# Reordering the end of each retention group: gate products, outputs and output transposes

## The chip, the cores and the metric

The kernel runs on one core of a Trainium2 chip. The metric is the device time of one execution in microseconds (us), lower is better; several executions are timed and their median is compared. The engines are named as in the profile: PE is TensorE, DVE is VectorE, ACT is ScalarE, POOL is GpSimd, SP is SyncE, which here only issues DMAs.

## The reference

One layer of a bidirectional encoder, 1024 tokens by 1024 features, float32. After a modulated RMS norm, one input projection feeds two head groups. Group A is retention: 8 heads with 64-wide q and k and 128-wide v, each in chunks of 128 tokens, a forward and a backward direction, then a group norm per head and a SiLU gate. Group B is latent attention. Both go through one output projection. The change touches group A and the gate of group B:

```
rq, rk = rope(r_q), rope(r_k) * dk ** -0.5
scores = einsum('bhnik,bhnjk->bhnij', qc, kc) * decay_intra
out    = einsum('bhnij,bhnjv->bhniv', scores, vc) + (qc * q_decay) @ states   # chunkwise, both directions
o      = (o - mean(o)) * rsqrt(var(o) + EPS) * ret_gn_w                       # per head, over its 128 columns
ret_out = o * silu(r_g)
mla_out = rms_norm(att) * silu(m_g)
```

## The kernel before

All large products are made in three parts, from high and low halves of both operands: mm3 (L64 to L67) issues high x high (L65), high x low (L66) and low x high (L67). The normalised input is held as hh[k] and hl[k], k = 0 to 7 (128 features by 1024 tokens each); weight pages are loaded by SP, split by ACT (L80) and POOL (L81) and held in a ring of 7.

Retention works in four groups g of two heads (the loop at L333). In each group:

- For each of eight token tiles t, 24 products (8 k by 3 parts, 512 columns) make q, k and v of the tile in one acc bank. ACT copies v out (L348); DVE multiplies q and k by the cosine and sine tables into t1 and t2 (L357, L359), two buffers each; POOL sums them into one of two rotary buffers rb (L363, L364). Then comes the retention step of the tile: PE transposes q, k and a copy into a bank tp of tag sm (L372, L373), DVE and ACT make the halves (L375 to L385), PE makes the scores scp (mm3, L387) and the chunk's states kv (L394), in a bank of tag sm each, and DVE and ACT carry the states on (L389 to L410). In group 0 the products of all eight tiles are already made in the start stage.
- The gate: two heads by two halves of the tokens, 24 products each into an acc bank (in the profile `acc<-hh,wh`; a retention product is `acc<-wh,hh`), then ACT's Silu into sg (L423). sg has one buffer.
- The outputs, for each half of the tokens: four tiles, each with four matmuls into a bank op of tag sm (L433, L434), ACT's copy to o (L436, five buffers), DVE's statistics (L439, L440); POOL makes the power -0.5 (rstd, L61 and L62); DVE normalises in eight instructions (L446); PE transposes eight blocks into two tp banks of tag sm (L451); DVE multiplies with weight and gate into ro (L453, two buffers); SP stores ro to retD in DRAM (L455).

After the four groups, mla_gate(0) and mla_gate(1) make the gates of the attention heads in the same way, 24 products to an acc bank and a Silu into mo (L469), stored by ACT's queue (L470). For these two, mo has the tag ro: it shares the two buffers with the ro of the outputs.

PSUM has eight banks: four of tag acc, four of tag sm.

The order in which each engine issues its instructions is set by a planner when the program is built. It goes through the program by priority, which is the order of the source, takes what its own model holds ready, and fixes the order; each engine then follows its own queue in order, and waits at the head. A tile of a tag gets one of the tag's buffers when one is free. So in the profile products of later stages run ahead of earlier stages' waiting work: the gate products of a group at its beginning, and those of the next group's tiles between the retention steps.

`tc.issue_after(ins)` adds an edge of order alone: what the block issues on the engine of `ins` is queued behind `ins`.

Of the kernel before, what the change touches and what calls it, by code (L numbers as in the profile page):

```python
# [9 lines left out]
F32 = mybir.dt.float32  # L10
# [3 lines left out]
ALU = mybir.AluOpType  # L14
# [4 lines left out]
P = 128  # L19
D = 1024  # L20
S = 1024
KT = D // P
# [8 lines left out]
def body(tc, I, O):  # L31
    nc = tc.nc
    V, A, G, T, SY = nc.vector, nc.scalar, nc.gpsimd, nc.tensor, nc.sync
# [16 lines left out]
    ident = ctile("ident", P)  # L50
# [13 lines left out]
    def mm3(out, lh, ll, rh, rl, first, last, **kw):  # L64
        T.matmul(out, lh, rh, start=first, stop=False, **kw)  # L65
        T.matmul(out, lh, rl, start=False, stop=False, **kw)  # L66
        T.matmul(out, ll, rh, start=False, stop=last, **kw)  # L67

    p_lat = None
    s_h = ExitStack()  # L70
# [24 lines left out]
    def sm(n=512):  # L95
        return pp.tile([P, n], F32, name="sm", tag="sm", bufs=8 - NACC)

    hh = [p_h.tile([P, S], F32R, name=f"hh{k}", tag=f"hh{k}") for k in range(KT)]
    hl = [p_h.tile([P, S], F32R, name=f"hl{k}", tag=f"hl{k}") for k in range(KT)]
# [3 lines left out]
    ts_ = lambda t: slice(t * P, (t + 1) * P)  # L103
# [162 lines left out]
    for h in range(H):  # L266
# [17 lines left out]
                    in1=posf.unsqueeze(2).broadcast_to([P, NT, 32]), op=ALU.mult)  # L284
# [44 lines left out]
    for z_ in qz:  # L329
        for b_ in z_:  # L330
            G.memset(b_.bitcast(F32), 0.0)

    for g in range(4):  # L333
        w = w0 if g == 0 else [wpage(I["w_ret"][g][j], 1024, 2) for j in range(4)]
        vv = []
# [3 lines left out]
        for t in range(NT):  # L339
            if g == 0 and t < NB0:  # L340
                ps = acc0[t]
            else:
                ps = acc()
                for k in range(KT):
                    wh, wl = w[k // 2]
                    mm3(ps, hh[k][:, ts_(t)], hl[k][:, ts_(t)], wh[:, k % 2], wl[:, k % 2], k == 0, k == KT - 1)
            v_ = p_ret.tile([P, 2, P], F32, name="v", tag="v", bufs=9)
            A.copy(out=v_.rearrange("p h d -> p (h d)"), in_=ps[:, 256:512])  # L348
            vv.append(v_)
            xq = ps[:, 0:256]  # L350
            if g == 0 and NACC <= t < NB0:
                xq = p_ret.tile([P, 256], F32, name="xq", tag="o", bufs=5)
                A.copy(out=xq, in_=ps[:, 0:256])
            xq = xq.rearrange("p (a d) -> p a d", d=32)
            t1 = p_ret.tile([P, 4, 2, 32], F32, name="t1", tag="t1", bufs=2)
            t2 = p_ret.tile([P, 4, 2, 32], F32, name="t2", tag="t2", bufs=2)
            V.tensor_tensor(out=t1.rearrange("p a b d -> p (a b) d"), in0=xq,  # L357
                            in1=Cr[:, t:t + 1].broadcast_to([P, 8, 32]), op=ALU.mult)
            V.tensor_tensor(out=t2.rearrange("p a b d -> p (a b) d"), in0=xq,  # L359
                            in1=Sr[:, t:t + 1].broadcast_to([P, 8, 32]), op=ALU.mult)  # L360
            r_ = rbuf[t % 2]
            rv = r_.rearrange("p (a z) d -> p a z d", z=2)[:, :, 0].rearrange("p a (b d) -> p a b d", b=2)
            G.tensor_tensor(out=rv[:, :, 0], in0=t1[:, :, 0], in1=t2[:, :, 1], op=ALU.subtract)  # L363
            G.tensor_tensor(out=rv[:, :, 1], in0=t1[:, :, 1], in1=t2[:, :, 0], op=ALU.add)  # L364
            V.tensor_copy(out=r_[:, 1:6:2], in_=r_[:, 0:5:2])
            kd = p_ret.tile([P, 2, 2, 64], F32, name="kd", tag="kd", bufs=2)
            V.tensor_tensor(out=kd, in0=r_[:, 4:7:2].unsqueeze(2).broadcast_to([P, 2, 2, 64]),
                            in1=kfac[:, 2 * g:2 * g + 2].unsqueeze(3).broadcast_to([P, 2, 2, 64]), op=ALU.mult)

            tp = sm(384)  # L370
            for h in range(2):
                T.transpose(tp[:, ts_(h)], r_[:, 2 * h:2 * h + 2].rearrange("p a b -> p (a b)"), ident)  # L372
            T.transpose(tp[:, ts_(2)], r_[:, 5:7].rearrange("p a b -> p (a b)"), ident)  # L373
            qdT_ = p_ret.tile([P, 2, P], F32, name="qdT", tag="qdT", bufs=8)
            V.tensor_tensor(out=qdT_, in0=tp[:, 0:256].rearrange("p (a b) -> p a b", a=2),  # L375
                            in1=qfac[:, 2 * g:2 * g + 2], op=ALU.mult)

            kTh, kTl = (p_ret.tile([P, P], F32R, name=f"kT{n}", tag=f"kT{n}", bufs=1) for n in "hl")
            A.copy(out=kTh, in_=tp[:, 256:384])
            V.tensor_tensor(out=kTl, in0=tp[:, 256:384], in1=kTh, op=ALU.subtract)  # L380
            qh_, ql_ = qz[t % 2]
            for h in range(2):
                hs = slice(64 * h, 64 * h + 64)
                A.copy(out=qh_[hs, h], in_=tp[hs, ts_(h)])
                V.tensor_tensor(out=ql_[hs, h], in0=tp[hs, ts_(h)], in1=qh_[hs, h], op=ALU.subtract)  # L385
            scp = sm(256)
            mm3(scp, kTh, kTl, qh_.rearrange("p a b -> p (a b)"), ql_.rearrange("p a b -> p (a b)"), True, True)  # L387
            sT_ = p_ret.tile([P, 2, P], F32, name="sT", tag="sT", bufs=8)
            V.tensor_tensor(out=sT_, in0=scp.rearrange("p (h d) -> p h d", h=2), in1=mask[:, 2 * g:2 * g + 2],  # L389
                            op=ALU.mult)  # L390
            sT[t], qdT[t] = sT_, qdT_
            kv = sm(256)
            for h in range(2):
                T.matmul(kv[:, ts_(h)], kd[:, h].rearrange("p a b -> p (a b)"), v_[:, h], start=True, stop=True)  # L394
            kvv = kv.rearrange("p (h d) -> p h d", h=2)
            if t < NT - 1:
                if t == 0:
                    V.tensor_copy(out=ST[0:64, 1], in_=kvv[0:64])
                else:
                    for h in range(2):  # L400
                        V.scalar_tensor_tensor(out=ST[0:64, t + 1, h], in0=ST[0:64, t, h],
                                               scalar=gch[0:64, 2 * g + h:2 * g + h + 1], in1=kvv[0:64, h],
                                               op0=ALU.mult, op1=ALU.add)
            if t > 0:
                A.copy(out=ST[64:128, t - 1], in_=kvv[64:128])
# [6 lines left out]

        wg = [wpage(I["w_rg"][g][j], 1024, 4) for j in range(2)]
        sg = p_ret.tile([P, 2, S], F32, name="sg", tag="sg")
        for h in range(2):
            for half in range(2):
                ps = acc()
                for k in range(KT):
                    wh, wl = wg[k // 4]
                    rh = hh[k][:, half * 512:half * 512 + 512]  # L420
                    rl = hl[k][:, half * 512:half * 512 + 512]
                    mm3(ps, wh[:, k % 4, ts_(h)], wl[:, k % 4, ts_(h)], rh, rl, k == 0, k == KT - 1)
                A.activation(sg[:, h, half * 512:half * 512 + 512], ps, AF.Silu)  # L423

        for half in range(2):
            mv = p_ret.tile([P, 4, 2, 2], F32, name="mv", tag="mv", bufs=2)
            ob = []
            for q in range(4):
# [15 lines left out]
            for q in range(4):  # L444
                for h in range(2):
                    V.tensor_scalar(out=ob[q][:, h], in0=ob[q][:, h], scalar1=mv[:, q, h, 0:1],  # L446
                                    scalar2=rst[:, q, h:h + 1], op0=ALU.subtract, op1=ALU.mult)
            for h in range(2):
                tp = sm()
                for q in range(4):  # L450
                    T.transpose(tp[:, ts_(q)], ob[q][:, h], ident)  # L451
                ro = p_ret.tile([P, 512], F32, name="ro", tag="ro", bufs=2)
                V.scalar_tensor_tensor(out=ro, in0=tp, scalar=gnw[:, 2 * g + h:2 * g + h + 1],  # L453
                                       in1=sg[:, h, half * 512:half * 512 + 512], op0=ALU.mult, op1=ALU.mult)
                SY.dma_start(out=retD[2 * g + h, :, half * 512:half * 512 + 512], in_=ro)  # L455


    def mla_gate(n, pool, tag):
        wg = [wpage(I["w_mg"][n][j], 1024, 4) for j in range(2)]
        for h in range(2):  # L460
            for half in range(2):
                ps = acc()
                sl = slice(half * 512, half * 512 + 512)
                for k in range(KT):
                    wh, wl = wg[k // 4]
                    mm3(ps, wh[:, k % 4, ts_(h)], wl[:, k % 4, ts_(h)], hh[k][:, sl], hl[k][:, sl],
                        k == 0, k == KT - 1)
                mo = pool.tile([P, 512], F32, name=tag, tag=tag, bufs=2)
                A.activation(mo, ps, AF.Silu)  # L469
                A.dma_start(out=mgD[2 * n + h, :, sl], in_=mo)  # L470
# [430 lines left out]
WLX = (6, 7)  # L901
XDVE, KACT = (3, 6), 1
MG0 = 2
EARLY = (2, 6)
TWO_PI = 2 * np.pi
PI_IN = 3.1415925
# [68 lines left out]
```

## Time and profile before

| | us |
|---|---|
| median of 3 runs | 1119.9 |
| lowest, highest | 1119.32, 1124.02 |
| the profiled execution | 1122.44 |
| its span, first to last instruction | 1120.5 |
| PE busy in the span | 1037.8 |
| mean granted clock of PE, as a share of 2.4 GHz | 0.96 |

In the profile's rows a time is counted from the span's start. Groups 0 to 3 end at about 184, 288, 387 and 475 us. "Busy" of PE counts a pipelined matmul from its start to its modelled end, so busy PE is not PE at its best; the granted clock stands beside it. A wait is given with the instruction whose end released it.

### The profile page before, as it was taken

The numbers are of one execution on the slowest core, as the hardware profiler recorded it, in microseconds if no ns is written. First come the engines' busy times: TensorE is split into PE (matmuls) and PEld (weight loads), VectorE is DVE, ScalarE is ACT, GpSimd is POOL, SyncE is SP. The second block draws the span as 40 slices with busy tenths as digits, with TensorE's granted clock in tenths as the row PEclk, the third lists the DMA queues.
The fourth block names the chain that finished last, engine by engine and source line by source line (L and its number), as shares of the span: only waits on it lengthen the run. The fifth ranks groups of instructions, "written<-read, shape, count | busy, mean of one in ns | idle before, by whom it ended". The sixth has DMA issues, their size and how long they took to land.

```text
span 1120.5 us, 15200 instructions
## 1 busy us (share of the span) xinstructions
PE 1037.8 (93%) x5672; PEld 899.8 (80%) x5672; DVE 586.6 (52%) x1390; ACT 430.2 (38%) x864; POOL 408.5 (36%) x313
## 2 busy tenths in 40 slices
PE   5899988988798898599999999998999999998998
PEld 5678876877687687489988888987889999887887
DVE  7984364434445444503540211676777777875332
ACT  6663122213121222112442201666776777773100
POOL 3244114203221421111554311784445665764310
PEclk8899988999799899799999999999999999999999
DMA  9611003101110200121545452010000000003432
GB/s 373 237 57 53 23 4 111 38 1 57 57 38 1 99 21 26 44 92 53 181 157 169 160 186 86 1 39 1 20 1 20 20 20 20 20 3 119 146 110 75
DMA packets 30744, 82.27 MB, mean 73 GB/s; under 512 B 3536, under 2 KB 4560, under 8 KB 30672
## 3 DMA queue, kind: packets, MB, share of 16 engines
q1 hardware_dynamic: 25920, 72.92, 19.2%
q10 hardware_dynamic: 4752, 8.39, 2.0%
q8 instruction: 45, 0.74, 0.3%
q14 instruction: 27, 0.22, 0.1%
HBM read 64.52 MB, written 16.78 MB: 73 GB/s over the span
## 4 chain that ended last, share of the span: by engine, by line
PE 49%; DVE 4%; DMA 2%; ACT 1%; POOL 1%; issue 1%; ACTq 0%; DVEq 0%; POOLq 0%
PE acc L65 5%; PE acc L66 5%; PE acc L67 5%; PE pt L748 4%; PE sp L65 4%; PE sp L66 4%; PE sp L67 4%; PE po L66 3%; PE po L67 3%; PE po L65 3%; DMA wa<-w_ada 2%; PE sm L67 1%; PE sm L66 1%; PE sm L65 1%; PE pt L661 1%
## 5 line engine op out<-in xcount | busy, mean ns | idle before, releaser
L81 POOL TENSOR_TENSOR wl<-wr,wh 128x1024 fp32r<-128x1024 f32 (+2 forms) x51 | 114.7, 2256 | 204.1 <-ACT wh L80 188.3
L65 PE MATMUL acc<-wh,hh 128*128 128x512 f32 (+2 forms) x352 | 130.1, 370 | 1.7 <-ACT hh L189 1.7
L66 PE MATMUL acc<-wl,hh 128*128 128x512 f32 (+2 forms) x352 | 129.5, 368 | 0.0
L67 PE MATMUL acc<-wh,hl 128*128 128x512 f32 (+2 forms) x352 | 125.6, 365 | 1.2 <-DVE hl L190 1.2
L65 PE MATMUL acc<-hh,wh 128*128 128x512 f32 x256 | 106.1, 415 | 14.6 <-DVE t L359 6.9
L734 POOL TENSOR_SCALAR pr<-pr,st 128x1024 f32<-128x1024 f32 x62 | 72.4, 1170 | 102.1 <-DVE st L733 77.0
L66 PE MATMUL acc<-hl,wh 128*128 128x512 f32 x256 | 104.5, 408 | 0.0
L67 PE MATMUL acc<-hh,wl 128*128 128x512 f32 x256 | 103.7, 405 | 0.0
L751 DVE TENSOR_TENSOR pl<-pt,ph 128x512 fp32r<-128x512 f32 x128 | 85.2, 683 | 32.0 <-ACT ph L750 32.0
L80 ACT CAST wh<-wr 128x1024 fp32r<-128x1024 f32 (+2 forms) x55 | 53.7, 980 | 107.8 <-PE sm L66 55.0
L750 ACT CAST ph<-pt 128x512 fp32r<-128x512 f32 x128 | 73.1, 591 | 28.3 <-PE pt L748 26.3
L363 POOL TENSOR_TENSOR rb<-t,t 128x128 f32<-128x128 f32 x32 | 16.0, 501 | 179.8 <-PE sm L373 95.0
L729 DVE TENSOR_REDUCE st<-sp 128x1 f32<-128x1024 f32 x62 | 75.4, 1216 | 6.6 <-PE sp L67 6.5
L66 PE MATMUL po<-pl,vh 128*128 128x256 f32 x256 | 76.7, 300 | 2.1 <-DVE pl L751 2.0
L732 ACT ACTIVATE pr<-sp,st 128x1024 f32<-128x1024 f32 x62 | 69.5, 1120 | 19.3 <-DVE st L730 19.1
L65 PEld LDWEIGHTS acc<-wh,hh 128*128 128x128 f32 x352 | 67.0, 190 | 10.9 <-ACT hh L189 2.1
L748 PE MATMUL pt<-ident,pr 128*128 128x128 f32 x496 | 70.6, 275 | 5.0 <-DVE st L733 2.7
L66 PEld LDWEIGHTS acc<-wl,hh 128*128 128x128 f32 x352 | 67.0, 190 | 8.9
L67 PEld LDWEIGHTS acc<-wh,hl 128*128 128x128 f32 x352 | 66.0, 188 | 10.0 <-DVE hl L190 1.6
L65 PE MATMUL po<-ph,vh 128*128 128x256 f32 x256 | 73.7, 288 | 0.0
L65 PEld LDWEIGHTS acc<-hh,wh 128*128 128x128 f32 x256 | 50.7, 198 | 27.9 <-DVE t L359 7.8
L67 PE MATMUL po<-ph,vl 128*128 128x256 f32 x256 | 73.1, 286 | 0.0
(363 smaller groups left out, 2538.4 us busy)
## 6 DMA issues: line engine op xcount, KB each, us to landing
x<-w_ada SPq DMA_DIRECT2D x16, 512.0 KB, 6.6
wr<-w_ret SPq DMA_DIRECT2D x16, 512.0 KB, 3.5
wr<-w_rg SPq DMA_DIRECT2D x8, 512.0 KB, 3.5
retD<-ro SPq DMA_DIRECT2D x16, 256.0 KB, 2.1
wr<-w_mg SPq DMA_DIRECT2D x8, 512.0 KB, 3.6
wa<-w_ada SPq DMA_DIRECT2D x8, 512.0 KB, 3.5
wr<-w_out SPq DMA_DIRECT2D x8, 512.0 KB, 4.2
wro<-retD SPq DMA_DIRECT2D x8, 512.0 KB, 4.6
```

The costliest lines, as they stand in the source:

```text
L65: T.matmul(out, lh, rh, start=first, stop=False, **kw)
L66: T.matmul(out, lh, rl, start=False, stop=False, **kw)
L67: T.matmul(out, ll, rh, start=False, stop=last, **kw)
L80: A.copy(out=hi, in_=raw)
L81: eng.tensor_tensor(out=lo, in0=raw, in1=hi, op=ALU.subtract)
L363: G.tensor_tensor(out=rv[:, :, 0], in0=t1[:, :, 0], in1=t2[:, :, 1], op=ALU.subtract)
L729: V.tensor_reduce(out=st_[:, 0:1], in_=sp, op=ALU.max, axis=AX.X)
L732: A.activation(pr, sp, AF.Exp, bias=st_[:, 1:2], scale=sc_, accum_out=st_[:, 2:3])
L734: G.tensor_scalar(out=pr, in0=pr, scalar1=st_[:, 3:4], scalar2=0.0, op0=ALU.mult, op1=ALU.add)
L748: T.transpose(tp[:, ts_(q)], pr[:, ts_(half * 4 + q)], ident)
L750: A.copy(out=ph[half][:, :, c_], in_=tv)
L751: V.tensor_tensor(out=pl[half][:, :, c_], in0=tv, in1=ph[half][:, :, c_], op=ALU.subtract)
```

## The change

The outputs of the first half are written ahead of the gate's second head; the function outputs(half) now ends with the normalisation and puts the rest (transposes, multiply, store) into a list, pending. turn_outputs(last) takes the oldest of the list and issues it with its PE instructions queued behind `last`. For half 0 that is the last product of gate(1) of its own group, for half 1 the last product of tile 1 (PEND) of the next group. In group 3, half 1's is the last product of the first tile of the second head in mla_gate(0). mm3 returns its last matmul for this.

```diff
@@ -64,7 +64,7 @@
     def mm3(out, lh, ll, rh, rl, first, last, **kw):
         T.matmul(out, lh, rh, start=first, stop=False, **kw)
         T.matmul(out, lh, rl, start=False, stop=False, **kw)
-        T.matmul(out, ll, rh, start=False, stop=last, **kw)
+        return T.matmul(out, ll, rh, start=False, stop=last, **kw)
 
     p_lat = None
     s_h = ExitStack()
@@ -330,6 +330,13 @@
         for b_ in z_:
             G.memset(b_.bitcast(F32), 0.0)
 
+    pending = []
+
+    def turn_outputs(last):
+
+        with tc.issue_after(last.ins):
+            pending.pop(0)()
+
     for g in range(4):
         w = w0 if g == 0 else [wpage(I["w_ret"][g][j], 1024, 2) for j in range(4)]
         vv = []
@@ -343,7 +350,9 @@
                 ps = acc()
                 for k in range(KT):
                     wh, wl = w[k // 2]
-                    mm3(ps, hh[k][:, ts_(t)], hl[k][:, ts_(t)], wh[:, k % 2], wl[:, k % 2], k == 0, k == KT - 1)
+                    last = mm3(ps, hh[k][:, ts_(t)], hl[k][:, ts_(t)], wh[:, k % 2], wl[:, k % 2], k == 0, k == KT - 1)
+                if pending and t == PEND:
+                    turn_outputs(last)
             v_ = p_ret.tile([P, 2, P], F32, name="v", tag="v", bufs=9)
             A.copy(out=v_.rearrange("p h d -> p (h d)"), in_=ps[:, 256:512])
             vv.append(v_)
@@ -412,17 +421,18 @@
 
         wg = [wpage(I["w_rg"][g][j], 1024, 4) for j in range(2)]
         sg = p_ret.tile([P, 2, S], F32, name="sg", tag="sg")
-        for h in range(2):
+        def gate(h):
             for half in range(2):
                 ps = acc()
                 for k in range(KT):
                     wh, wl = wg[k // 4]
                     rh = hh[k][:, half * 512:half * 512 + 512]
                     rl = hl[k][:, half * 512:half * 512 + 512]
-                    mm3(ps, wh[:, k % 4, ts_(h)], wl[:, k % 4, ts_(h)], rh, rl, k == 0, k == KT - 1)
+                    last = mm3(ps, wh[:, k % 4, ts_(h)], wl[:, k % 4, ts_(h)], rh, rl, k == 0, k == KT - 1)
                 A.activation(sg[:, h, half * 512:half * 512 + 512], ps, AF.Silu)
-
-        for half in range(2):
+            return last
+
+        def outputs(half):
             mv = p_ret.tile([P, 4, 2, 2], F32, name="mv", tag="mv", bufs=2)
             ob = []
             for q in range(4):
@@ -445,14 +455,23 @@
                 for h in range(2):
                     V.tensor_scalar(out=ob[q][:, h], in0=ob[q][:, h], scalar1=mv[:, q, h, 0:1],
                                     scalar2=rst[:, q, h:h + 1], op0=ALU.subtract, op1=ALU.mult)
-            for h in range(2):
-                tp = sm()
-                for q in range(4):
-                    T.transpose(tp[:, ts_(q)], ob[q][:, h], ident)
-                ro = p_ret.tile([P, 512], F32, name="ro", tag="ro", bufs=2)
-                V.scalar_tensor_tensor(out=ro, in0=tp, scalar=gnw[:, 2 * g + h:2 * g + h + 1],
-                                       in1=sg[:, h, half * 512:half * 512 + 512], op0=ALU.mult, op1=ALU.mult)
-                SY.dma_start(out=retD[2 * g + h, :, half * 512:half * 512 + 512], in_=ro)
+
+            def finish(g=g, sg=sg):
+                for h in range(2):
+                    tp = sm()
+                    for q in range(4):
+                        T.transpose(tp[:, ts_(q)], ob[q][:, h], ident)
+                    ro = p_ret.tile([P, 512], F32, name="ro", tag="ro", bufs=2)
+                    V.scalar_tensor_tensor(out=ro, in0=tp, scalar=gnw[:, 2 * g + h:2 * g + h + 1],
+                                           in1=sg[:, h, half * 512:half * 512 + 512], op0=ALU.mult, op1=ALU.mult)
+                    SY.dma_start(out=retD[2 * g + h, :, half * 512:half * 512 + 512], in_=ro)
+            pending.append(finish)
+
+        gate(0)
+        outputs(0)
+        last = gate(1)
+        turn_outputs(last)
+        outputs(1)
 
 
     def mla_gate(n, pool, tag):
@@ -463,8 +482,10 @@
                 sl = slice(half * 512, half * 512 + 512)
                 for k in range(KT):
                     wh, wl = wg[k // 4]
-                    mm3(ps, wh[:, k % 4, ts_(h)], wl[:, k % 4, ts_(h)], hh[k][:, sl], hl[k][:, sl],
-                        k == 0, k == KT - 1)
+                    last = mm3(ps, wh[:, k % 4, ts_(h)], wl[:, k % 4, ts_(h)], hh[k][:, sl], hl[k][:, sl],
+                               k == 0, k == KT - 1)
+                if pending and h:
+                    turn_outputs(last)
                 mo = pool.tile([P, 512], F32, name=tag, tag=tag, bufs=2)
                 A.activation(mo, ps, AF.Silu)
                 A.dma_start(out=mgD[2 * n + h, :, sl], in_=mo)
@@ -901,6 +922,7 @@
 WLX = (6, 7)
 XDVE, KACT = (3, 6), 1
 MG0 = 2
+PEND = 1
 EARLY = (2, 6)
 TWO_PI = 2 * np.pi
 PI_IN = 3.1415925
```

## Rows read from the trace of the kernel before

**Rows 1.** Page, part 1: busy us (share of span) xinstructions

```profile
PE 1037.8 (93%) x5672; PEld 899.8 (80%) x5672; DVE 586.6 (52%) x1390; ACT 430.2 (38%) x864; POOL 408.5 (36%) x313
```

**Rows 2.** Windows: stretch, us, each engine's busy us, PE clock, DMA share, GB/s

```profile
176.35:194.26 17.91, 12.39 (x46) 9.19 (x45) 9.48 (x21) 3.79 (x8) 8.92 (x7) 0.71 0.36 119
276.60:297.71 21.11, 11.50 (x46) 9.09 (x45) 8.25 (x30) 3.67 (x10) 8.46 (x8) 0.68 0.26 85
379.63:396.40 16.77, 11.38 (x46) 8.44 (x45) 9.41 (x22) 3.53 (x8) 7.91 (x7) 0.80 0.33 102
440.40:474.99 34.59, 18.53 (x98) 15.70 (x97) 20.20 (x79) 5.90 (x18) 5.10 (x5) 0.78 0.14 47
197.00:240.00 43.00, 43.00 (x216) 36.49 (x215) 17.42 (x50) 9.58 (x25) 10.06 (x12) 1.00 0.08 25
```

**Rows 3.** Waits of PE: releaser, us in total, times, longest

```profile
PE sm L451 <- DVE o L446: 20.4, 6, 7.3
```

**Rows 4.** Timeline of PE, end of group 0: start, us, instruction [idle before]

```profile
172.63 0.48 PE L434 MATMUL sm<-ST,qdT 64*128 64x128 f32 x2
...
173.62 0.39 PE L65 MATMUL acc<-wh,hh 128*128 128x512 f32 x1
...
176.12 0.39 PE L67 MATMUL acc<-wh,hl 128*128 128x512 f32 x1
178.77 0.65 PE L451 MATMUL sm<-ident,o 128*128 128x128 f32 x2 [2.27 <-DVE o L446]
179.26 0.40 PE L372 MATMUL sm<-ident,rb 128*128 128x128 f32 x2
...
183.90 0.79 PE L65 MATMUL acc<-hh,wh 128*128 128x512 f32 x1 [2.55 <-DVE t L359]
...
191.82 0.28 PE L65 MATMUL sm<-qzh,kTh 128*128 128x256 f32 x1
...
192.87 0.48 PE L66 MATMUL acc<-hl,wh 128*128 128x512 f32 x1
...
194.26 0.50 PE L65 MATMUL acc<-hh,wh 128*128 128x512 f32 x1 [0.69 <-ACT sg L423]
```

**Rows 5.** Timeline of PE, end of group 1

```profile
276.12 0.48 PE L434 MATMUL sm<-ST,qdT 64*128 64x128 f32 x2
283.88 0.80 PE L451 MATMUL sm<-ident,o 128*128 128x128 f32 x2 [7.28 <-DVE o L446]
284.47 0.63 PE L372 MATMUL sm<-ident,rb 128*128 128x128 f32 x2
...
288.25 0.79 PE L65 MATMUL acc<-hh,wh 128*128 128x512 f32 x1 [1.65 <-DVE t L359]
...
297.71 0.50 PE L65 MATMUL acc<-hh,wh 128*128 128x512 f32 x1 [0.69 <-ACT sg L423]
```

**Rows 6.** Timeline of PE, end of group 2

```profile
381.59 0.65 PE L451 MATMUL sm<-ident,o 128*128 128x128 f32 x2 [1.80 <-DVE o L446]
```

**Rows 7.** Timelines of DVE and ACT, end of group 0

```profile
176.36 4.46 DVE L446 TENSOR_SCALAR o<-o,mv,rst 128x128 f32<-128x128 f32 x8 [2.05 <-POOL rst L62]
...
183.44 0.41 DVE L359 TENSOR_TENSOR t<-acc,Sr 128x256 f32<-128x256 f32 x1
...
193.62 0.60 ACT L423 ACTIVATE sg<-acc 128x512 f32<-128x512 f32 x1 [9.28 <-PE acc L67]
```

**Rows 8.** Timeline of DVE, end of group 1

```profile
283.48 2.14 DVE L446 TENSOR_SCALAR o<-o,mv,rst 128x128 f32<-128x128 f32 x8 [4.78 <-POOL rst L62]
```

**Rows 9.** Timelines of DVE, ACT and PE, end of group 3

```profile
463.03 1.41 DVE L453 SCALAR_TENSOR_TENSOR ro<-sm,small,sg 128x512 f32<-128x512 f32 x2
...
474.34 0.60 ACT L469 ACTIVATE ro<-acc 128x512 f32<-128x512 f32 x1 [8.39 <-DMA retD<-ro]
...
474.99 0.79 PE L65 MATMUL acc<-hh,wh 128*128 128x512 f32 x1 [3.58 <-ACT ro L469]
```

**Rows 10.** Page, part 6: stores of ro, KB each, us from issue to landing

```profile
retD<-ro SPq DMA_DIRECT2D x16, 256.0 KB, 2.1
```

## The prediction

> **What bounds the kernel now.** I read the page's busy shares first: TensorE (PE) is busy 93% of the span, every other engine about half of it or less [rows 1]. Time can then only come from stretches in which PE stands still or runs at a low clock, and the table of windows shows these among the stages that the diff touches [rows 2]. In the middle of group 1 PE is busy for all 43.00 us at a granted clock of 1.00. At the ends of groups 0, 1 and 2 it is busy 12.39 of 17.91, 11.50 of 21.11 and 11.38 of 16.77 us, with the clock at 0.68 to 0.80, and at the end of group 3 it is busy 18.53 of 34.59 us. The list of waits says for whom: 20.4 us in six waits of the output transposes (L451) for VectorE's normalisation (L446), group 3's among them [rows 3].
>
> The order on PE at the end of group 0 [rows 4] shows how this comes about. The last output product of the second half is at 172.63; products of group 1's tile 7 follow until 176.12; then PE waits 2.27 us for the first two transposes. Only behind these come group 1's own first transposes (L372, 179.26), although they stand ahead of the products of tile 7 in the program. The same order, two L451 and then L372, stands at the end of group 1, after a wait of 7.28 us [rows 5]; group 2 stops likewise for 1.80 us [rows 6]. I read it as an order of banks: tiles of tag sm get their banks in program order, so tp of the next group's tile 0 comes behind the two tp of the outputs, and these wait for normalised data. From L372 runs the next chain: it frees a rotary buffer for GpSimd's sums (L363), these free the operands of VectorE's L357 and L359, which read tile 4 out of its bank (end at 183.85) [rows 7], and at 183.90 the first gate product starts, released by L359 [rows 4]. All four acc banks hold group 1's tiles 4 to 7 until then. The second gate tile waits for ScalarE's Silu of the first (193.62) and starts at 194.26 [rows 4, 7].
>
> **The change part by part.** No product, copy, transpose or DMA is added or removed; the sum is one of order.
>
> *Outputs of half 0 ahead of gate(1).* The gate products of a group already run at its beginning: those of group 1 from 183.90, its outputs until 276.60 [rows 4, 5]. So this, and the edge that queues the half 0 transposes behind gate(1), bind nothing: 0. Were the gate products not done by then, they would be the filler that PE lacks, which excludes a loss.
>
> *Half 1's transposes, multiply and store behind the next group's products of tile 1.* Those products, too, are done before the outputs (tile 7 is at 176.12), so the edge binds nothing. What moves is the program order: the next group's tp, scores and kv of tile 0 now get their sm banks ahead of the two tp of the outputs, and PE need not stand at L451. The first L372 can follow the last output product: 173.1 instead of 179.26, 276.6 instead of 284.47 [rows 4, 5]. L363, L357, L359 and the release of the first acc bank come forward with it, and gate products fill the wait for the normalisation. The stores move back on SP's queue by as much as their data; nothing but a ro buffer waits for them.
>
> The price per end: between the last product before the stop and the second gate tile lie 24 gate products at 0.227 us (11 steps in 2.50 us), the ten instructions of one retention step in 1.05 us (191.82 to 192.87), and eleven transposes at that step's mean of 0.105 us: 5.4 + 1.1 + 1.2 = 7.7 us of work [rows 4]. The windows are 17.91, 21.11 and 16.77 us long [rows 2], so 10.2, 13.4 and 9.1 us are lost, low clock and waits together. If the chain comes early enough, all of it can go in groups 0 and 2: in group 0 the normalisation ends at 180.82, and transposes (0.8), two multiplies (1.41) and the Silu (0.60) lead to 183.6 [rows 7, 9], while PE's queued work from 173.04 (3.3 us of products and the 7.7) ends at 184.0, against 194.26. At the end of group 1 the normalisation ends only at 285.62 [rows 8], and the same steps lead to 288.4; with the first products at a low clock I say 289.2 instead of 297.71: 8.5 us.
>
> *Half 1's end of group 3 behind the first product tile of the second head in mla_gate(0).* There PE stops because four finished mla_gate(0) tiles fill the acc banks: their Silu needs a buffer of tag ro, and these also go in program order, behind all four ro of the outputs. ScalarE sits 8.39 us until a store of retD has landed, and PE starts at 474.99 [rows 9]. After the change two of the mo tiles stand ahead of the last two ro. The first two ro are computed from 463.03 to 464.44 [rows 9] and land 2.1 us later [rows 10]; 0.60 us of Silu gives a bank at 467.1, and 48 products (10.9 us) then cover the rest of the outputs. That is 7.9 us, less about 0.4 for transposes that now share PE's time: 7.5.
>
> *Sum.* 10.2 + 8.5 + 9.1 + 7.5 = 35.3 us is the most. Against it stands that each queue's order is fixed ahead of the run: where the late transposes are queued too early, PE still stands for the normalisation. The bounds are nothing and today's three waits, 2.27 + 7.28 + 1.80 = 11.4 us [rows 4, 5, 6]; I take half, 5.7, since one gate tile now may lie before the transposes but need not all be queued before them. The gate's Silu now waits for the late multiplies, because sg has one buffer: between nothing and three times today's wait of 0.69 us for that Silu [rows 4], I take 1. So 35.3 - 6.7 = 28.6 us. The profiled execution took 1122.4 us (span 1120.5, 1.9 around it): 1093.8. The median of the runs is 2.5 us below the profiled one, so on its scale 1091.
>
> A row to weigh: the eight normalisations took 4.46 us at the end of group 0 against 2.14 at group 1's [rows 7, 8]. The Trainium skill, SBUF — State Buffer, section "SBUF: two separate sides", says that VectorE and GpSimd share one port pair as an exclusive lock, so that the later one blocks for a whole instruction. By that rule a weight page of GpSimd's that slides into group 1's normalisation would cost some 2.3 us there, and one that slides out of group 0's would give as much back; no run here shows which, and the sum stands without it.
>
> **The rivals.**
>
> *A: the bank takes the transposes' place.* L372 comes early, but L357 and L359 are queued behind all eight normalisations on VectorE, so tile 4's bank comes free only after them. For it: L359 is already the releaser at 183.90 and 288.25 [rows 4, 5]. Against it: VectorE stands idle for 4.78 us ahead of group 1's normalisation [rows 8]. The gate would start 0.8 us (two of 0.41) after 180.82 and 285.62, so at 181.6 and 286.4 instead of 183.90 and 288.25, some 2 us for each of three ends; with group 3's 7.5 the gain is 13.5 us: 1106. The Trainium skill, Perfetto Trace Analysis, section "Optimization Strategy", holds that one gap coming back on the busy engine can mean too few SBUF or PSUM buffers; the repeated stop with full banks agrees, and by that rule a change of order alone gives no more than A.
>
> *B: slower, the late transposes come too late.* They now queue for sm banks behind the next group's scores, and ro, the single sg, the gate's Silu and the acc banks wait for them. It decides when the late multiplies end after today's Silu begins, 193.62 in group 0: 10.5 us after the 183.1 that their data allow. Were they to come two retention steps with 34 products later (8.8 us each), each of three ends would lose about 7 us, less 7.5 at group 3: 13.5 us, 1133. Against it: VectorE's and ScalarE's pieces between L372 and the scores are short, and the normalisation is done soon after them.
>
> *C: no change.* If L372's place is due to readiness and not to banks, PE's order stays: 1120. Against it: L372 stands in the same odd place, between L451, at the ends of groups 0 and 1.
>
> **How the numbers follow.** My forecast, 1081 to 1099, has 0.64; A (1099 to 1112) 0.18; C 0.09; B 0.09. The likeliest is 1091. The range leaves out B and C and reaches over A's middle: 1081 to 1110; below, 35.3 us on the median's scale would be 1084.6, and I add 3.6 us for waits inside the retention steps. A measurement of this kernel can tell about 0.5%, 5.6 us, from no change. Faster by more: 0.82; within: 0.09; slower: 0.09.
>
> **What would show it.** Right: L372 ahead of every L451 of half 1 at the ends of groups 0 to 2; those L451 between gate products; the windows there full and at a clock near 1.00; at group 3 products right after the first two stores have landed; waits of L451 for L446 under 8 us in all. A shows a gate product waiting for L359 right after an early L372; B shows gate products waiting for the Silu of sg, and that for L453. Wrong altogether: a different number of products between the retention steps inside a group, or an L372 still behind L451.

## The result, and the profile after

| | before | after |
|---|---|---|
| median, us | 1120.53 | 1103.82 |
| lowest, highest | 1119.32, 1124.02 | 1102.52, 1106.24 |
| executions | 4 | 4 |
| profiled execution, its span | 1122.44, 1120.5 | 1102.52, 1100.4 |

The changed kernel takes 0.9848 of the time before (95% interval 0.982 to 0.9877). That is 16.7 us, inside the range given and on the side given, where 28.6 us were forecast. The change moved L372 to L381 (a step's transposes), L384 to L393 (qzh), L423 to L432 (the gate's Silu), L446 to L456 (normalisation), L451 to L463 (output transposes), L453 to L465 (ro), L469 to L490 (Silu into mo) and L549 to L570 (transposes of cn, the first PE work of the next stage).

The page's busy shares answer to [rows 1]: the same 5672 matmuls, in 7.1 us less busy time.

```profile
PE 1030.7 (94%) x5672; PEld 896.7 (81%) x5672; DVE 587.4 (53%) x1390; ACT 430.1 (39%) x864; POOL 408.7 (37%) x313
```

The windows, columns as in [rows 2]: three from the first transposes of the next group to its second gate tile, and the last from the last product of mla_gate(0) to the first product of mla_gate(1), across group 3's outputs. PE now has nearly the same busy time in stretches that end earlier, but it still stands for 3.7, 5.1 and 6.6 us, and in two of the three its clock is still near 0.8.

```profile
170.62:186.22 15.60, 11.92 (x61) 9.52 (x60) 11.70 (x27) 5.23 (x10) 11.16 (x10) 1.00 0.46 147
269.95:285.81 15.86, 10.73 (x46) 8.69 (x45) 8.88 (x31) 3.48 (x10) 8.31 (x8) 0.78 0.27 87
369.80:387.64 17.84, 11.20 (x46) 8.65 (x45) 10.03 (x31) 3.67 (x10) 7.62 (x8) 0.81 0.21 67
431.33:458.22 26.89, 15.88 (x92) 13.79 (x90) 15.20 (x65) 6.02 (x18) 3.85 (x5) 0.81 0.14 42
```

The list of PE's waits says what changed places. The output transposes wait 6.7 us for the normalisation where [rows 3] had 20.4. The gate's products wait 5.5 us for the Silu of sg, three times, where before each such wait was 0.69 us [rows 4, 5]. And the scores of tile 0 wait 19.6 us for ScalarE's qzh; the same row of the kernel before, shown last, has 12.9 us in 6.

```profile
PE sm L65 <- ACT qzh L393: 19.6, 8, 3.4
PE sm L463 <- DVE o L456: 6.7, 2, 5.2
...
PE acc L65 <- ACT sg L432: 5.5, 3, 2.0
```

```profile
PE sm L65 <- ACT qzh L384: 12.9, 6, 2.7
```

PE's timeline at the end of group 1 answers to [rows 5]. L381 follows the last output product at once, 14.5 us earlier than before (269.95 against 284.47). Then the scores of tile 0 come next in the queue and stand 3.33 us for qzh. Eighteen and six gate products follow, at first 0.43 us apart and later 0.23. Only then, at 282.65, come the eight output transposes, and the second gate tile starts at 285.81.

```profile
269.54 0.48 PE L444 MATMUL sm<-ST,qdT 64*128 64x128 f32 x2
269.95 0.44 PE L381 MATMUL sm<-ident,rb 128*128 128x128 f32 x2
...
273.83 0.58 PE L65 MATMUL sm<-qzh,kTh 128*128 128x256 f32 x1 [3.33 <-ACT qzh L393]
274.21 1.05 PE L403 MATMUL sm<-v,kd 128*128 128x128 f32 x4
274.92 0.77 PE L65 MATMUL acc<-hh,wh 128*128 128x512 f32 x1
275.49 0.63 PE L66 MATMUL acc<-hl,wh 128*128 128x512 f32 x1
...
280.80 0.39 PE L67 MATMUL acc<-hh,wl 128*128 128x512 f32 x1
...
281.25 0.40 PE L65 MATMUL acc<-hh,wh 128*128 128x512 f32 x1
...
282.42 0.39 PE L67 MATMUL acc<-hh,wl 128*128 128x512 f32 x1
282.65 0.71 PE L463 MATMUL sm<-ident,o 128*128 128x128 f32 x5
...
285.81 0.50 PE L65 MATMUL acc<-hh,wh 128*128 128x512 f32 x1 [1.80 <-ACT sg L432]
```

VectorE and ScalarE beside it show that the transposes are late, not their data [rows 8]. The eight normalisations end at 279.92 (277.78 + 2.14). VectorE then waits for PE's transposes, and ScalarE's Silu of the first gate tile, whose products were done at 282.8, waits for VectorE's two multiplies, since the one sg buffer is theirs until 285.1 (283.72 + 1.41).

```profile
277.78 2.14 DVE L456 TENSOR_SCALAR o<-o,mv,rst 128x128 f32<-128x128 f32 x8 [1.54 <-POOL rst L62]
...
283.72 1.41 DVE L465 SCALAR_TENSOR_TENSOR ro<-sm,small,sg 128x512 f32<-128x512 f32 x2 [1.84 <-PE sm L463]
...
285.16 0.60 ACT L432 ACTIVATE sg<-acc 128x512 f32<-128x512 f32 x1 [11.38 <-DVE ro L465]
```

PE at the ends of groups 0 and 2 and ScalarE and PE at the end of group 3 complete the picture. At the third end the scores stop PE for 3.36 us, and their second product for 1.59 more. At group 3 the first product of mla_gate(1) starts at 458.22, released by the first Silu into mo, 2.42 us after the last output product began (455.80); before it was 9.98 us (465.01 to 474.99, [rows 9]). ScalarE's third Silu into mo still sits 10.34 us for a store, but PE has work then.

```profile
170.62 0.44 PE L381 MATMUL sm<-ident,rb 128*128 128x128 f32 x2
...
182.64 0.84 PE L463 MATMUL sm<-ident,o 128*128 128x128 f32 x3 [1.47 <-DVE o L456]
...
186.22 0.50 PE L65 MATMUL acc<-hh,wh 128*128 128x512 f32 x1 [2.00 <-ACT sg L432]
...
373.71 0.39 PE L65 MATMUL sm<-qzh,kTh 128*128 128x256 f32 x1 [3.36 <-ACT qzh L393]
...
376.13 0.58 PE L66 MATMUL sm<-qzl,kTh 128*128 128x256 f32 x1 [1.59 <-DVE qzl L394]
...
387.64 0.50 PE L65 MATMUL acc<-hh,wh 128*128 128x512 f32 x1 [1.70 <-ACT sg L432]
...
455.80 0.48 PE L444 MATMUL sm<-ST,qdT 64*128 64x128 f32 x2
458.22 0.50 PE L65 MATMUL acc<-hh,wh 128*128 128x512 f32 x1 [1.94 <-ACT ro L490]
```

```profile
457.57 0.60 ACT L490 ACTIVATE ro<-acc 128x512 f32<-128x512 f32 x1 [0.83 <-DMA retD<-ro]
...
469.63 0.60 ACT L490 ACTIVATE ro<-acc 128x512 f32<-128x512 f32 x1 [10.34 <-DMA retD<-ro]
```

So in the profiles the second gate tiles came 8.0, 11.9 and 8.8 us earlier at the three ends (194.26, 297.71 and 396.40 against 186.22, 285.81 and 387.64), each counted from the start, and from the third of them to the first transposes of cn (515.91 before, 497.98 after) another 9.2 us went: 17.9 in all. The rest of the two spans' difference of 20.1 lies behind, where the code is the same; the profiled executions are 19.9 us apart, the medians 16.7.

The lead shrinks from 11.9 to 8.8 us between the second and the third end. In the kernel before, 16 products of the next group's tiles stood behind group 2's last output product (375.87 to 379.40). In the changed kernel they are used up ahead of it, and nothing fills the stop for the scores. The same holds at the end of group 1; at the end of group 0, 14 such products (170.93 to 174.00) cover that time.

### The profile page after: what moved, and what is told of

Read it like the earlier page. It is cut to its first block, busy times and chain, and to the rows that moved or that the text cites. A ratio compares the mean times of both kernels' runs of the same rounds, so it can differ in the third digit from the quotient of the medians.

```text
span 1100.4 us, 15201 instructions
## 1 busy us (share of the span) xinstructions
PE 1030.7 (94%) x5672; PEld 896.7 (81%) x5672; DVE 587.4 (53%) x1390; ACT 430.1 (39%) x864; POOL 408.7 (37%) x313
## 3 DMA queue, kind: packets, MB, share of 16 engines
q1 hardware_dynamic: 25920, 72.92, 19.6%
## 4 chain that ended last, share of the span: by engine, by line
PE 75%; DVE 13%; DMA 3%; ACT 3%; issue 3%; POOL 2%; ACTq 0%; SPq 0%; POOLq 0%; DVEq 0%
PE acc L65 12%; PE acc L66 12%; PE acc L67 12%; PE pt L769 4%; PE sp L65 4%; PE sp L67 4%; PE sp L66 4%; PE po L66 3%; PE po L67 3%; PE po L65 3%; PE sm L65 2%; DVE x L178 2%; PE sm L66 2%; PE sm L67 2%; DMA wa<-w_ada 2%
## 5 line engine op out<-in xcount | busy, mean ns | idle before, releaser
L65 PE MATMUL acc<-hh,wh 128*128 128x512 f32 x256 | 103.8, 405 | 9.4 <-ACT sg L432 5.5
L66 PE MATMUL acc<-hl,wh 128*128 128x512 f32 x256 | 102.1, 399 | 0.0
L372 POOL TENSOR_TENSOR rb<-t,t 128x128 f32<-128x128 f32 x32 | 15.6, 488 | 168.5 <-PE sm L382 108.8
```

## The experiments

Each kernel is an edit of the changed kernel (e5: of the one before). All compute the whole reference. Kernels that share a median of the kernel before ran on the same chip.

| run | median, us (lowest, highest) | kernel before | ratio, 95% interval |
|---|---|---|---|
| e1 | 1110.41 (1109.52, 1110.72) | 1119.1 | 0.9921 [0.9906, 0.9936] |
| e2 | 1113.17 (1112.14, 1116.26) | 1119.1 | 0.9952 [0.9936, 0.9967] |
| e3 | 1090.46 (1089.04, 1090.92) | 1119.1 | 0.9742 [0.9726, 0.9758] |
| e4 | 1105.36 (1103.39, 1106.51) | 1119.1 | 0.9875 [0.9861, 0.989] |
| e5 | 1120.73 (1119.0, 1122.84) | 1120.43 | 1.0005 [0.9995, 1.0015] |
| e6 | 1108.8 (1108.36, 1108.88) | 1120.43 | 0.9895 [0.988, 0.991] |
| e7 | 1095.98 (1095.45, 1096.64) | 1120.43 | 0.9782 [0.9766, 0.9798] |
| e8 | 1088.02 (1087.33, 1091.62) | 1120.43 | 0.9717 [0.9698, 0.9736] |
| e9 | 1096.67 (1093.48, 1096.98) | 1119.61 | 0.9786 [0.9762, 0.981] |
| e10 | 1090.06 (1089.12, 1092.4) | 1119.61 | 0.9738 [0.972, 0.9757] |

**e1, the bank order undone.** Half 1's end goes behind tile 0's products, ahead of tile 0's transposes; group 3 stays as changed.

```diff
-PEND = 1
+PEND = 0
```

> PEND is 0: half 1's transposes stand behind the next group's products of tile 0, and so ahead of that tile's transposes, scores and kv in the program; group 3 stays as changed. Main theory (the ends of groups 0 to 2 gain by the order of sm banks, some 7 us by the profile at the second gate tile of group 2's end; group 3 by the order of the ro buffers, some 9 us): L372's counterpart stands behind two output transposes again, the wait of the transposes for the normalisation is back near 11 us at these ends, and the time is 1109 to 1113. Rival 1 (all of the gain is group 3's): 1104. Rival 2 (all of it is the bank order): 1120.

8.7 us below the kernel before: the main theory's range. PE's waits show the old stop again, with L381 behind two L463. So half 1's place in the program, ahead of tile 0's transposes or behind them, is what put L372 there. That the place acts through the order of the sm banks is argued: it also sets the priority by which the planner goes, and no run parts the two.

```profile
PE sm L463 <- DVE o L456: 16.4, 5, 7.0
```

```profile
283.16 0.79 PE L463 MATMUL sm<-ident,o 128*128 128x128 f32 x2 [7.01 <-DVE o L456]
283.75 0.63 PE L381 MATMUL sm<-ident,rb 128*128 128x128 f32 x2
```

**e2, group 3 undone.** Its half 1 is finished at once; groups 0 to 2 stay as changed.

```diff
         turn_outputs(last)
         outputs(1)
+        if g == 3:
+            turn_outputs(last)
```

> Half 1's end of group 3 is issued at once, ahead of mla_gate(0); groups 0 to 2 stay as changed. Main theory: ScalarE waits for the store of the last ro again before the first mo, PE starts after group 3 about 8 us later against the last output product, and the time is 1111 to 1114. Rival 1 (all of the gain is group 3's): 1120. Rival 2 (all is the bank order): 1104.

5.9 us below the kernel before, as the main theory had it. The first product of mla_gate(1) again waits for a Silu into mo that comes behind the stores (469.83, 10.2 us after the last output product began); that Silu waits 8.59 us for a store of ro. The two parts add up: 8.7 + 5.9 = 14.6 us, against 16.7 for the changed kernel and 13.7 for e4, whose order is the same.

```profile
469.83 0.79 PE L65 MATMUL acc<-hh,wh 128*128 128x512 f32 x1 [3.79 <-ACT ro L492]
```

**e3, sg in four tiles.** The same bytes, handed out as four tiles of one head and one half each, so that the first gate tile's Silu needs only the quarter that half 0 has long left.

```diff
-        sg = p_ret.tile([P, 2, S], F32, name="sg", tag="sg")
+        sg = {}
...
-                A.activation(sg[:, h, half * 512:half * 512 + 512], ps, AF.Silu)
+                sg[h, half] = p_ret.tile([P, 512], F32, name="sg", tag="sg", bufs=4)
+                A.activation(sg[h, half], ps, AF.Silu)
...
-                                           in1=sg[:, h, half * 512:half * 512 + 512], op0=ALU.mult, op1=ALU.mult)
+                                           in1=sg[h, half], op0=ALU.mult, op1=ALU.mult)
```

> sg is four tiles of 512 columns (tag sg, four buffers, the same space), so that the Silu of the next group's first gate tile overwrites only what half 0 has already used. Main theory (what the ends of groups 0 to 2 still lose behind the early transposes is the wait of the gate's Silu, and with it of the acc bank, for the late multiplies of half 1): the three waits of a gate product for the Silu, 5.5 us, go, and the time falls by 4 to 6 us, to 1098 to 1100. Rival (the scores of tile 0 at the head of PE's queue set the ends, and the gate tile waits for another bank next): within 1.5 us of 1104.

Far past what was expected of it: 13 to 15 us below the changed kernel (1103.82; e4, with the same order on PE and on e3's chip, 1105.36) instead of 4 to 6. In ScalarE's timeline the Silu at the end of group 0 starts at 181.53 (185.57 after the change), and in PE's the second gate tile at the end of group 1 starts at 279.34, where the changed kernel has 285.81. From 160 to 400 us PE waits for sg only there, 0.69 us. Of the waits that are left, the third fence has the longest in total, that for qzh.

```profile
181.53 0.60 ACT L433 ACTIVATE sg<-acc 128x512 f32<-128x512 f32 x1
```

```profile
279.34 0.50 PE L65 MATMUL acc<-hh,wh 128*128 128x512 f32 x1 [0.69 <-ACT sg L433]
```

```profile
PE sm L65 <- ACT qzh L393: 15.4, 7, 3.1
```

The expectation had counted the 5.5 us of waits by name and not what else hangs on them. The first transposes of cn come 12.3 us earlier than in the changed kernel (485.7 against 497.98). But the edit removed more than the Silu's wait, for PE's queue got another order. At the ends of groups 1 and 2, 12 and 17 products of the next group's tiles now stand behind the early transposes, where the changed kernel has none. The scores behind them find qzh ready, so both of their stops (3.33 and 3.36 us) are gone, and from the first transposes to the second gate tile the granted clock is 1.00 at all three ends (0.78 and 0.81 at two of them in the changed kernel). The 13 to 15 us are the price of the single sg with all of this; no run parts the Silu's wait from the scores' stops, and the expectation's rival, which named the scores, is not refuted by e3.

```profile
265.95 0.27 PE L382 MATMUL sm<-ident,rb 128*128 128x128 f32 x1
...
268.60 0.39 PE L67 MATMUL acc<-wh,hl 128*128 128x512 f32 x1
268.83 0.28 PE L65 MATMUL sm<-qzh,kTh 128*128 128x256 f32 x1
```

**e4, no edges, both gates first.** Neither issue_after nor the order gate(0), outputs(0), gate(1).

```diff
-        with tc.issue_after(last.ins):
-            pending.pop(0)()
+        pending.pop(0)()
...
         gate(0)
-        outputs(0)
         last = gate(1)
+        outputs(0)
```

> No issue_after edge, and gate(0) and gate(1) both ahead of the outputs of half 0; the deferral stays. Main theory (edges and the order of gate(1) and outputs(0) bind nothing): 1104, within 3 us. Rival (the explicit edges are what orders PE): back to 1115 or more.

As the changed kernel. The edges and the order of gate and outputs bind nothing; all of the gain comes from where half 1's end stands in the program.

At this point a second theory, called X in the expectations, stood: sg is the one lock that ate the gain, so that without it the order of banks gives about what was forecast; on the other hand sg in parts alone gives nothing, and a later turn with a single sg makes things worse. Its rivals put the gain down to room as such, or to where the turn is.

**e5, sg in four tiles in the kernel before.** The edit of e3, on before.

> The kernel before with sg as four tiles and nothing else. Theory X (the single sg binds only once half 1's multiplies are deferred behind the next group's first step): no change, 1119 within 2 us. Theory Y (the single sg cost its time before too, and the four tiles gain by themselves): about 1105, as much below the kernel before as the four tiles gained on the changed kernel.

No change, as X says: in the old order a gate product waits 0.69 us for the Silu at each of the three ends, with sg single and in four tiles alike (2.1 us in all in both), so there the Silu never waited for sg.

**e6, sg in four tiles and the bank order undone.** e3 with PEND = 0.

> The changed kernel with sg as four tiles and PEND 0, so that the output transposes get their sm banks ahead of the next group's first step again. Theory X: as without the four tiles, 1110 within 2 us, so that the bank order is worth about 20 us at the ends of groups 0 to 2 once sg does not hold it back, near the 27.8 - 5.7 that the prediction had. Theory Y: about 1097.

As X says. Between e6 and e3 only the order of banks differs: 0.9895 against 0.9742, or some 17 to 18 us with sg out of the way, where it is 5.9 us with a single sg (e2). Here too the name "order of banks" stands for half 1's place in the program.

**e7, sg in four tiles, half 1's end right behind tile 0's transposes.** Ahead of tile 0's scores and kv.

```diff
-                if pending and t == PEND:
-                    turn_outputs(last)
...
-            T.transpose(tp[:, ts_(2)], r_[:, 5:7].rearrange("p a b -> p (a b)"), ident)
+            last = T.transpose(tp[:, ts_(2)], r_[:, 5:7].rearrange("p a b -> p (a b)"), ident)
+            if pending and t == 0:
+                turn_outputs(last)
```

> sg as four tiles; half 1's transposes, multiply and store stand right behind the next group's first transposes (tile 0), ahead of its scores and kv in bank order. Theory X (the early transposes of tile 0 bring the gain; behind them the output transposes may stand either side of the scores): within 3 us of 1090. Rival (PE waits for the normalisation again with the scores behind it): 1095 to 1105.

5 us slower than e3, in the rival's range; theory X's is missed. What is new is one wait at the end of group 2, where the first gate product stands 6.89 us for VectorE's read-out of tile 4 (L366). Here no products of the next group's tiles are left behind the first transposes (in e3, 17), and the read-out (367.23) comes ahead of the normalisation (368.35), behind GpSimd's weight subtraction and rotary sums and a slow copy of VectorE's (L372, 1.87 us). So the wait is not for the outputs. What in e7's order took the 17 products away is not shown, nor that too early a place costs by itself.

```profile
360.54 0.27 PE L380 MATMUL sm<-ident,rb 128*128 128x128 f32 x1
367.70 0.79 PE L65 MATMUL acc<-hh,wh 128*128 128x512 f32 x1 [6.89 <-DVE t L366]
```

**e8, sg in four tiles and half 1's end behind tile 2's products.** e3 with PEND = 2.

> sg as four tiles and PEND 2: half 1's transposes stand one retention step later still in the program. Theory X (what is late with half 1 now is the second gate tile's sg buffer and the o buffers, and a step of 8.8 us more brings the Silu wait back): 1095 to 1105. Rival (nothing waits for the late part any more): within 3 us of 1090.

The fastest of all, 32.4 us below the kernel before. The rival's range holds and theory X's (1095 to 1105) is missed. It is 2.4 us below e3, but the two ratios' intervals overlap, so whether it is faster than e3 stays open.

**e9, a single sg and PEND = 2.** The changed kernel with that one constant.

> The changed kernel with its single sg and PEND 2: half 1's multiplies one retention step later still. Theory X (the single sg is what the lateness of the multiplies is paid through; rival B of the prediction as a mechanism): each of three ends waits longer for the gate's Silu, in all 5 to 25 us more than the changed kernel, 1109 to 1129. Rival (the four tiles gain by something else than the Silu's wait for the late multiplies): within 3 us of 1104, or as much below it as PEND 2 was with four tiles.

Here theory X fell: with sg single, a later turn makes the kernel 7 to 9 us faster than the changed one, not slower. The rival's two figures are missed as well. Its timeline at the end of group 1 shows why. Tile 1's transposes (276.31) now stand ahead of the outputs', so tile 5's bank comes free too: 27 gate products run from 282.35 to 288.29, which makes 43 ahead of the outputs' transposes where the changed kernel has 24, while two Silus wait together until 291.90. The scores' stops are still there (3.64 and 3.44 us). What the order costs is seen once, at group 0: a gate product stands 5.49 us for tile 5's read-out, which VectorE has queued behind the eight normalisations.

```profile
276.31 0.63 PE L381 MATMUL sm<-ident,rb 128*128 128x128 f32 x2
...
282.35 0.39 PE L66 MATMUL acc<-hl,wh 128*128 128x512 f32 x1
...
288.29 0.39 PE L65 MATMUL acc<-hh,wh 128*128 128x512 f32 x1
...
289.31 1.04 PE L463 MATMUL sm<-ident,o 128*128 128x128 f32 x8
```

```profile
291.90 1.08 ACT L432 ACTIVATE sg<-acc 128x512 f32<-128x512 f32 x2 [1.23 <-DVE ro L465]
```

```profile
187.57 0.79 PE L65 MATMUL acc<-hh,wh 128*128 128x512 f32 x1 [5.49 <-DVE t L368]
```

**e10, sg in four tiles and PEND = 3.**

> sg as four tiles and PEND 3, one step later than the last. Theory X (four tiles give the late part room for one more gate tile, after which the second gate tile's Silu and the o buffers wait): slower than PEND 2 with four tiles, 1092 to 1105. Rival (no wait ends on the late part any more): within 3 us of 1088.

Within 3 us of e8, as the rival had it; theory X's 1092 to 1105 is missed. One gate product stands 4.86 us for the Silu of sg (278.34), but sg does not hold that Silu: ScalarE has it (277.68) behind the copy to kTh, which waits for VectorE's eight normalisations (6.61 us from 269.37). From the second tile on, no difference between the places is clear of noise while sg is in four tiles.

Put together, in medians of us (1105.4 is e4, with the order of PEND = 1; the last row is from two chips):

| | single sg | sg in four tiles |
|---|---|---|
| PEND = 0 | 1110.4 | 1108.8 |
| PEND = 1 | 1103.8, 1105.4 | 1090.5 |
| PEND = 2 | 1096.7 | 1088.0 |

## Why the prediction was right in kind and wrong in size

**What bounds the kernel, and by what order.** Right in what was shown: PEND alone moves L381 from behind the output transposes to the last output product (e1 against the changed kernel), and the edges move nothing (e4). Rival C is out. That the order goes by banks and not by the planner's priority stays argued.

**Outputs of half 0, and the edges: 0.** Right (e4).

**Group 3: 7.5 us.** From the second gate tile of group 2's end to the first transposes of cn the profiles give 119.51 us before and 110.34 after: 9.2. The runs give 8.7 (e1). The step was right and 1 to 2 us small.

**The ends of groups 0 to 2: 27.8 us, less 6.7.** This is where the forecast failed: 21.1 us were expected, and the runs gave 5.9 (e2), the profiles 8.8 up to the third end. The step that failed is the term for the gate's Silu, "because sg has one buffer: between nothing and three times today's wait of 0.69 us for that Silu [rows 4], I take 1". Sg in parts is worth 13 to 15 us (e3 against the changed kernel and e4), the scores' stops that went with it included. The term's upper bound was taken from a wait in the old order. There the late multiplies were done at 182.46 (181.07 + 1.39, the row below), long before the Silu was due at 193.62 [rows 7], and sg in parts is worth nothing (e5).

```profile
181.07 1.39 DVE L453 SCALAR_TENSOR_TENSOR ro<-sm,small,sg 128x512 f32<-128x512 f32 x2
```

In the new order PE has, at the end of group 1, 24 gate products and then nothing until a bank comes free. Either of two things frees one: the Silu of the finished gate tile, which needs sg, which needs the late multiplies; or tile 5's read-out, which needs tile 1's transposes, and these stand among the output transposes in PE's queue (283.19 to 283.74). Both chains run through the output transposes at 282.65. Cutting the first (e3) or the second (e9) gave 13 to 15 and 7 to 9 us; cutting both (e8) 16 to 17. So the lost gain went in large part into one lock with two doors, and either door opens it in part. How much of the rest is the scores' is the next point but one.

**"Queued too early": 5.7 us.** Wrong in kind. At the three ends the output transposes waited only 1.47 us for the normalisation (group 0); of the 6.7 us of that row 5.2 is the one wait at group 3. They were queued too late instead: at the end of group 1 their data were ready at 279.92 and they were issued at 282.65; at the third end 379.91 and 384.58. Only at the end of group 0 were the data late, since the normalisation took 5.92 us there. That is rival B's mechanism in small. B was weighed against the old Silu at 193.62, and by that measure 10 us of slack were left; it should have been weighed against the moment at which PE runs out of banks in the new order, which the forecast itself had at 184.0.

**The scores at the head of the queue.** Not in the sum at all. With tile 0's transposes early, its scores come early too, and PE stands for qzh 19.6 us instead of 12.9; the 6.7 us more are the stops of 3.33 and 3.36 us at the ends of groups 1 and 2. After the first of them eight products came 0.43 us apart (275.49 to 278.90) at a granted clock of 0.50, the level of 1.2 GHz, against 0.23 later (281.25 to 282.42) at 1.00: 0.2 x 8 = 1.6 us on top. In the profiles of the changed kernel, e3, e8, e9 and e10, PE stands for qzh behind the early transposes at just those ends where no products of the next group's tiles are left to fill: at both in the changed kernel and e9, at group 2's in e8 (3.55 us) and e10 (3.65 us), at none in e3. The prediction counted such products as filler at the end of group 0 (3.3 us) and did not ask where they would stand at the other ends in the new order; why the planner spends them earlier in some versions is open.

**Rival A** (1106) came nearest in number, but not by its mechanism: no gate product waits for L368 in the changed kernel. A read-out queued behind the eight normalisations, as it described, is seen for tile 5 only, in e9 (5.49 us) and e8 (1.61 us); the gate's waits for a read-out in e3 (1.92 us) and e7 (6.89 us) end ahead of the normalisation. By the rule of the Trainium skill that was set beside it (Perfetto Trace Analysis, "Optimization Strategy": a bubble that keeps coming back can mean too few buffers), as the prediction read it, order alone should give no more than 13.5 us. It gave 16.7, and with PEND = 2 some 23 (e9). The rule pointed at the right place all the same: e3 frees a buffer, with not a byte more, only in four pieces.

**What would show it.** L381 ahead of L463 at the three ends, L463's waits under 8 us (6.7), and at group 3 products right after the first stores: right. L463 between gate products: only in that they follow some; PE runs dry behind them. Full windows at a clock near 1.00: wrong, 10.73 of 15.86 us busy at 0.78 in group 1. Gate products waiting for the Silu of sg, and that for the multiplies, had been named as B's mark, and they are what the profile shows.

**The forecast's number.** 28.6 us is what e3 gave (1119.1 to 1090.46), a coincidence and not the forecast's terms: e6 has 11.6 us without the bank order, and the bank order adds 17 to 18. The changed kernel itself missed the forecast's own interval, 1081 to 1099. That 1103.82 lies inside the range is luck as far as the groups' ends go: the range was drawn out over rival A, and A's mechanism did not occur.

## What to carry to other kernels

Where a planner goes by program order, in priority and in handing out the buffers of a tag, that order can act like a dependency: work written later can stand behind an earlier tile's wait. Here moving the earlier tile's work in the program gave all of the gain, and the edges of issue none. When work is deferred, list every single buffer and every bank that it goes on holding and what is left to fill the stops, and compare the time at which it lets go with the moment the bounding engine runs dry in the new order, not with a wait measured in the old. A buffer that is filled and read in parts should be handed out in parts: four sg tiles of the same total size changed nothing in the old order and 13 to 15 us in the new, and with PEND = 2 they make the fastest version here, 1088.0 us, 0.9717 of the time before.

## What the runs showed of the hardware beyond that

The same eight normalisations took 5.92 us at the end of group 0, and 2.14 and 2.13 us at the ends of groups 1 and 2. By form, one took 341 ns in the median and 2371 ns at most. GpSimd's timeline has two weight subtractions of 2.4 us in the slow stretch and none in the others.

```profile
177.18 5.92 DVE L456 TENSOR_SCALAR o<-o,mv,rst 128x128 f32<-128x128 f32 x8
```

```profile
176.79 2.40 POOL L81 TENSOR_TENSOR wl<-wr,wh 128x1024 fp32r<-128x1024 f32 x1
180.02 2.49 POOL L81 TENSOR_TENSOR wl<-wr,wh 128x1024 fp32r<-128x1024 f32 x1 [0.83 <-ACT wh L80]
```

```profile
L456 DVE TENSOR_SCALAR o<-o,mv,rst x64: 330/341/2371, 157.3 to 461.3; 128x128 f32<-128x128 f32 x64
```

In the kernel before it was 4.46 us at groups 0 and 2 (the row below) and 2.14 at group 1 [rows 7, 8]. So the reordering moved such a subtraction into the first of them and out of the third. A copy shows the same: beside a subtraction it took 1.88 us at the third end, where its median is 0.29, and it made PE's second scores product wait 1.59 us for qzl.

```profile
379.17 4.46 DVE L446 TENSOR_SCALAR o<-o,mv,rst 128x128 f32<-128x128 f32 x8 [2.04 <-POOL rst L62]
```

```profile
373.87 1.88 DVE L374 COPY rb<-rb 128x192 f32<-128x192 f32 x1 [0.51 <-POOL rb L373]
```

```profile
373.80 1.80 POOL L81 TENSOR_TENSOR wl<-wr,wh 128x768 fp32r<-128x768 f32 x1
```

The rows agree with the rule weighed ahead of the result (the Trainium skill, SBUF — State Buffer, "SBUF: two separate sides": the port pair that VectorE and GpSimd share is an exclusive lock, held for a whole instruction, between a GpSimd instruction and one of VectorE in a two-port mode or with two SBUF inputs). No row tells the mode of these instructions, and that this lock is the cause was not tried by itself. Nor does it explain the forecast's miss: in e3 the eight normalisations took 6.13, 5.45 and 5.80 us at the three ends, each beside two subtractions, and e3 is 13 to 15 us faster than the changed kernel.
